# Longer DRAM runs, a weight part on ScalarE, and gathered rows and early blocks moved to another stage, in a one-layer transformer trunk with product-key experts

## The chip, the cores and the metric

The kernel runs on one core of a Trainium2 chip. Its engines work side by side, each through an instruction queue of its own and in order: PE (TensorE, the matmuls, with PEld for its weight loads), DVE (VectorE), ACT (ScalarE), POOL (GpSimd, here the gathers) and SP (SyncE, here the queue of most loads). Sixteen DMA engines move the data. The metric is device microseconds (us) of one execution; the time of a kernel is the median of its runs.

## The reference

One layer over 1024 tokens of width 1024. A norm, one projection, differential attention beside an RG-LRU branch, an output projection, then the part that this change touches, a product-key expert layer (PEER):

```python
q = (xt @ w_query).reshape(T, PEER_HEADS, 2, PEER_HALF)        # 8 heads
s1, s2 = q[:, :, 0] @ sub_keys_1.T, q[:, :, 1] @ sub_keys_2.T   # 128 keys each
v1, i1 = top_k(s1, 16); v2, i2 = top_k(s2, 16)
sc, ci = top_k(all sums v1 + v2, 16)
eid = i1[ci // 16] * 128 + i2[ci % 16]                          # 1 of 16384 experts
g = softmax(sc)
out = sum over (h, k) of g * gelu(expert_down[eid] . xt) * expert_up[eid]
```

Each token so uses 128 of 16384 experts (8 heads, 16 each); `expert_down` and `expert_up` hold 1024 float32 per expert. A last norm follows.

## The kernel before

The 1024 tokens are split in two ways of computing the expert layer. The first 384 (three blocks, `NG = 3`) are **gathered**: POOL fetches one row of an expert table per token and slot (`row`, 128 tokens by 1024, 0.5 MB), and DVE multiplies it (L848 for `expert_down`, L858 for `expert_up`). There are 2 x 3 x 128 = 768 such rows. They are dealt out by hand as filler over the later stages: 45 in the attention of the second group, 30 in its output projection, `G_QRY` in its query stage, `G_OH` in the one-hot stage, and the rest (`G_UP`) in the up stage.

The other 640 tokens (five blocks, `ND = 5`) go **densely** through all 128 blocks of 128 experts, in these stages:

- **query stage**: query projection and the 16 largest keys (DVE, L597 to L601), then `top_k` for each of the five blocks, whose result `turn` transposes on PE (tile `ptk`).
- **one-hot stage**: a table of weights, 640 tokens by 16384 experts. For 16 tokens at a time `one_hots` builds one-hot rows on DVE (`o`, L1087) and multiplies them with the gate, which is split into three bfloat16 parts (`ov`, tile `o1v`, L1091). `weights` multiplies them on PE (tile `pg`, three matmuls per token), ACT copies the result to `st` (L1109), and it goes to DRAM (`gw_d`).
- **up stage**: for each block `e` of experts, `weigh` takes the activations `ga` (640 tokens), multiplies them with the weights `gw` of block `e` read back from DRAM (L1155), and splits the product in two float32r halves. Then 15 matmuls per output half (tile `pu`) add the block's part. `EG = 8` blocks make a group, and each group has two passes (one per output half); in the second pass the eight blocks of the next group are weighed, one after the other.

The activations `ga` come from `down_all(e)`: 48 matmuls (tile `pd`) with the block's `expert_down` weights (`draw`, split to `dh` by ACT, L124, and `dl` by DVE, L125) and a gelu by ACT (L997). Some of these blocks are computed **early**, in the query and one-hot stages, as filler for PE; their `ga` goes to DRAM (`act`) and is loaded again in the up stage. `EARLY` and `EXTRA` say which blocks are early (71 of them), `E_QRY`, `E_TOPK` and `E_OH` how many are handed out per stage, and `HOLD` how many of the last stay in SBUF.

A scheduler sets each engine's order from the program; the rows' DVE instructions are pinned in program order. `gw` has `EQ = 4` blocks per load and two buffers; `uraw` (expert_up) has three buffers.

Of the kernel before, what the change touches and what calls it, by code (L numbers as in the profile page):

```python
# [21 lines left out]
P = 128  # L22
# [21 lines left out]
EG = 8  # L44
EQ = 4
EARLY = 4
TG = 32
TB = 16
TI = 2

G_ATT, G_OUT, G_QRY, G_TOPK, G_OH = 45, 30, 70, 0, 128
G_UP = 2 * NG * SLOTS - (G_ATT + G_OUT + G_QRY + G_TOPK + G_OH)
B_OUT, B_CHAIN, B_TURN, B_QRY, B_TOPK = 0, 3, 8, 8, 12
A_STEPS, A_AHEAD, A_FILL, LRU_AT, WO_AT = 3, 4, 0.5, 0.7, 50
E_QRY, E_TOPK, E_OH = 8, 20, 40
TURN5 = 2
OH_LAST = 96
NORM_IN = ((0,), (1,), (2, 3))
NORM_B = ((0, 1), (2, 3))
HOLD = 2  # L60
PRE = 0
TAIL = 4
RAWS = 4
EXTRA = 8
E_FIRST = 32
# [36 lines left out]
def trunk(  # L102
    ctx: ExitStack,
    tc: tile.TileContext,
    x, norm1_g, w_qk, w_v, w_lru, lam4, subln_g, conv_w, conv_b, w_ra, b_ra, w_ri, b_ri,
    lru_lam, w_out, norm2_g, norm2_c, w_query, keys_t, down_t, expert_down, expert_up, norm_f_g, out,
):
# [872 lines left out]
    def down_all(e, pin=False):  # L980

        ga = dp.tile([P, TD], F32, name="ga", bufs=2 + HOLD + PRE)
        pd = [ps_d.tile([P, 512], F32, name="pd") for _ in range(2)]
        for kh in range(2):
            raw = dp.tile([P, 4, P], F32, name="draw", bufs=RAWS)
            nc.sync.dma_start(raw, down_t[e, :, 4 * kh:4 * kh + 4, :])
            wh = dp.tile([P, 4, P], F32R, name="dh")
            wl = dp.tile([P, 4, P], F32R, name="dl")
            split(raw, wh, wl)
            for c in range(2):  # L990
                sl = slice(c * HT, (c + 1) * HT)
# [14 lines left out]
    with ExitStack() as ph:  # L1006
# [29 lines left out]
        slot_k = [sl_pool.tile([P, P // TI, 2, TI], BF, name=f"slot_k{b}") for b in range(ND)]  # L1036
        slot_w = [sl_pool.tile([P, P // TI, 3, TI], BF, name=f"slot_w{b}") for b in range(ND)]
        ps_t = ph.enter_context(tc.tile_pool(name="ps_k", bufs=2, space=PSUM))
        def turn(b, five):
            pt = ps_t.tile([P, 5, P], BF, name="ptk")  # L1040
            for i in range(5):
                T.transpose(pt[:, i, :], five[:, i, :], ident_b)
            for dst, i, n in ((slot_k[b], 0, 2), (slot_w[b], 2, 3)):
                A.copy(dst.rearrange("p g n i -> p n g i"),
                       pt[:, i:i + n, :].rearrange("p n (g i) -> p n g i", i=TI))

        last = None
# [28 lines left out]
        def one_hots(t0):  # L1076


            b, tt = divmod(t0, P)
            g0 = tt // TI  # L1080

            def per_slot(t, n):
                return t[:, g0:g0 + GB, :, None, :].broadcast_to([P, GB, n, P, TI]).rearrange(
                    "p g n k i -> p (g n) k i")

            o = oh.tile([P, GB, 2, P, TI], BF, name="o21", bufs=3)
            V.tensor_tensor(o.rearrange("p g n k i -> p (g n) k i"),  # L1087
                            key_t[:, None, :, :].broadcast_to([P, GB * 2, P, TI]),
                            per_slot(slot_k[b], 2), op=ALU.is_equal)
            ov = oh.tile([P, GB, 3, P, TI], BF, name="o1v", bufs=OB)  # L1090
            V.tensor_tensor(ov.rearrange("p g n k i -> p g n (k i)"),  # L1091
                            o[:, :, 1:2, :, :].rearrange("p g n k i -> p g n (k i)").broadcast_to(
                                [P, GB, 3, P * TI]),
                            per_slot(slot_w[b], 3), op=ALU.mult)
            return o, ov

        def weights(t0, o, ov):
            if t0 % TG == 0:
                sts[t0 // TG] = st_pool.tile([P, NK, TG], F32, name="st")
            st = sts[t0 // TG]  # L1100
            for t4 in range(0, TB, 4):
                ps = ps_g.tile([P, 4, P], F32, name="pg")
                for t in range(t4, t4 + 4):
                    g, j = divmod(t, TI)
                    for i in range(3):
                        T.matmul(ps[:, t - t4, :], o[:, g, 0, :, j], ov[:, g, i, :, j],  # L1106
                                 start=i == 0, stop=i == 2)
# [23 lines left out]
    with ExitStack() as ph:  # L1131
        up = ph.enter_context(tc.tile_pool(name="up", bufs=2))
        wp = ph.enter_context(tc.tile_pool(name="wp", bufs=EG + 1))
        gp = ph.enter_context(tc.tile_pool(name="gp", bufs=2))
        ps_u = ph.enter_context(tc.tile_pool(name="ps_u", bufs=5, space=PSUM))
# [32 lines left out]
        for g in range(NK // EG):  # L1168
            for second in range(2):
# [100 lines left out]
```

## Time and profile before

| | |
|---|---|
| time, median of 3 runs | 2824.18 us (2811.93 to 2824.65) |
| the profiled execution's own time | 2816.51 us |
| its span, first to last instruction | 2814.6 us |
| PE busy in the span | 2644.4 us (94%) |
| DVE busy | 2336.4 us (83%) |
| ACT busy | 1041.5 us (37%) |
| mean granted TensorE clock | 0.974 |
| moved by DMA | 769.42 MB, mean 273 GB/s |

The stages that the change touches follow one another in the span: the query stage from 677 us to the first transpose of a top-k result at 954.7, the one-hot stage to 1470.9 (the last weight matmul), a switch to the first up matmul at 1509.5, and the up stage to 2803. An engine's busy time is what its instructions cover, and neighbouring matmuls overlap, so a pace is read from the count of matmuls in a stretch, not from the length of one.

### The profile page before, as it was taken

To read this page: it belongs to the slowest core of one execution; us is meant where nothing else is said; L and a number is where in the kernel's file an instruction comes from. 1 tells how busy PE (TensorE), PEld (TensorE's weight loads), DVE (VectorE), ACT (ScalarE), POOL (GpSimd) and SP (SyncE) were. 2 spreads that over 40 slices of the span, in tenths; PEclk is the share of its full clock that TensorE was granted. 3 is DMA by queue.
4 is the path that set the end of the run, shared out by engine and by line. 5 is a ranking of instruction groups with operands and counts; after the bars stand their busy time and mean duration, and the time that the engine had idled before them with its cause. 6 is when DMAs were issued, how large, how long until landed. Compare 5 with 4: busy or idle time off the path is not lost.

```text
span 2814.6 us, 43357 instructions
## 1 busy us (share of the span) xinstructions
PE 2644.4 (94%) x15489; PEld 2318.3 (82%) x15489; DVE 2336.4 (83%) x4838; ACT 1041.5 (37%) x1953; POOL 1119.6 (40%) x906
## 2 busy tenths in 40 slices
PE   7989978898998599999999999999999999999997
PEld 6765966647998599889998888888888888888886
DVE  7553979968999989999995888888888788888888
ACT  5652437824324444344342322222222222222222
POOL 2210035442250305643432444555464444545553
PEclk9999989999999799999999999999999999999999
DMA  6655389775583638888989999999999999999986
GB/s 196 148 140 174 110 200 233 227 266 207 187 291 112 199 105 311 329 297 311 345 320 363 313 324 330 346 338 347 336 332 318 316 336 332 356 340 332 342 292 235
DMA packets 353097, 769.42 MB, mean 273 GB/s; under 512 B 29696, under 2 KB 130064, under 8 KB 350320
## 3 DMA queue, kind: packets, MB, share of 16 engines
q0 software_dynamic: 136432, 425.67, 45.3%
q1 hardware_dynamic: 199488, 274.06, 29.6%
q10 hardware_dynamic: 16960, 66.92, 5.9%
q8 instruction: 121, 1.98, 0.3%
q14 instruction: 96, 0.79, 0.1%
HBM read 681.53 MB, written 85.00 MB: 272 GB/s over the span
## 4 chain that ended last, share of the span: by engine, by line
PE 66%; DVE 12%; issue 9%; DMA 8%; ACT 2%; POOL 2%; SPq 0%; ACTq 0%; POOLq 0%; DVEq 0%
PE pu L144 9%; PE pu L147 9%; PE pu L148 9%; PE pd L148 7%; PE pd L144 7%; PE pd L147 7%; PE pg L1106 3%; DVE row L848 3%; DMA row<-in_expert_down,eid 2%; POOL row L831 2%; PE pp L144 2%; PE pp L147 2%; PE pp L148 2%; PE pa L144 2%; PE pa L147 2%
## 5 line engine op out<-in xcount | busy, mean ns | idle before, releaser
L831 POOL DMA_INDIRECT row<-in_expert_up,eid x384 | 521.7, 1359 | 721.3 <-DVE accg L858 488.0
L831 POOL DMA_INDIRECT row<-in_expert_down,eid x384 | 518.0, 1349 | 548.7 <-DVE row L848 391.0
L144 PE MATMUL pd<-xdH,dh 128*128 128x320 f32 x2048 | 643.2, 315 | 5.3 <-ACT dh L124 3.5
L148 PE MATMUL pd<-xdH,dl 128*128 128x320 f32 x2048 | 628.9, 314 | 14.3 <-DVE dl L125 13.2
L147 PE MATMUL pd<-xdL,dh 128*128 128x320 f32 x2048 | 637.5, 312 | 0.0
L858 DVE SCALAR_TENSOR_TENSOR accg<-row,wg,accg 128x1024 f32<-128x1024 f32 x384 | 491.7, 1280 | 17.9 <-DMA row<-in_expert_up,eid 14.6
L147 PE MATMUL pu<-ul,w_h 128*128 128x512 f32 x1280 | 504.0, 394 | 0.2 <-DVE ul L125 0.2
L148 PE MATMUL pu<-uh,w_l 128*128 128x512 f32 x1280 | 500.3, 393 | 0.0
L848 DVE SCALAR_TENSOR_TENSOR row<-row,x2g 128x1024 f32<-128x1024 f32 x384 | 462.9, 1220 | 18.7 <-DMA row<-in_expert_down,eid 18.2
L148 PEld LDWEIGHTS pd<-xdH,dl 128*128 128x128 f32 x2048 | 386.0, 190 | 23.7 <-DVE dl L125 15.2
L144 PEld LDWEIGHTS pd<-xdH,dh 128*128 128x128 f32 x2048 | 390.0, 190 | 15.9 <-ACT dh L124 4.7
L147 PEld LDWEIGHTS pd<-xdL,dh 128*128 128x128 f32 x2048 | 389.3, 190 | 9.0
L144 PE MATMUL pu<-uh,w_h 128*128 128x512 f32 x1280 | 378.9, 394 | 11.2 <-ACT uh L124 5.8
L124 ACT CAST dh<-draw 128x512 fp32r<-128x512 f32 x256 | 159.0, 622 | 422.8 <-PE pd L147 390.4
L124 ACT CAST uh<-uraw 128x512 fp32r<-128x512 f32 x256 | 158.9, 621 | 416.8 <-PE pu L148 302.9
L147 PEld LDWEIGHTS pu<-ul,w_h 128*128 128x128 f32 x1280 | 242.0, 189 | 48.3 <-DVE ul L125 1.0
L148 PEld LDWEIGHTS pu<-uh,w_l 128*128 128x128 f32 x1280 | 242.1, 189 | 47.3
L144 PEld LDWEIGHTS pu<-uh,w_h 128*128 128x128 f32 x1280 | 236.0, 189 | 54.1 <-ACT uh L124 7.1
L125 DVE TENSOR_TENSOR dl<-draw,dh 128x512 fp32r<-128x512 f32 x256 | 174.6, 688 | 82.0 <-ACT dh L124 72.3
L125 DVE TENSOR_TENSOR ul<-uraw,uh 128x512 fp32r<-128x512 f32 x256 | 175.8, 687 | 42.1 <-ACT uh L124 40.3
L124 ACT CAST w_h<-ga 128x640 fp32r<-128x640 f32 x128 | 93.0, 730 | 260.8 <-PE pu L147 208.6
L997 ACT ACTIVATE ga<-pd 128x320 f32<-128x320 f32 x256 | 110.5, 435 | 142.2 <-PE pd L148 126.6
(262 smaller groups left out, 3948.9 us busy)
## 6 DMA issues: line engine op xcount, KB each, us to landing
draw<-in_down_t SPq DMA_DIRECT2D x256, 256.0 KB
uraw<-in_expert_up SPq DMA_DIRECT2D x256, 256.0 KB
gw<-gw_d SPq DMA_DIRECT2D x32, 1280.0 KB
gw_d<-st ACTq DMA_DIRECT2D x20, 1536.0 KB
act<-ga ACTq DMA_DIRECT2D x69, 320.0 KB
ga<-act SPq DMA_DIRECT2D x69, 320.0 KB
wraw<-in_w_query SPq DMA_DIRECT2D x64, 256.0 KB
gw_d<-st ACTq DMA_DIRECT2D x20, 512.0 KB
```

Source lines behind the costliest of these rows:

```text
L124: A.copy(hi, src)
L125: (eng or V).tensor_sub(lo, src, hi.bitcast(F32))
L144: t = T.matmul(ps, wh, mh, start=first, stop=False)
L147: T.matmul(ps, wh, ml, start=False, stop=False)
L148: T.matmul(ps, wl, mh, start=False, stop=last)
L831: nc.gpsimd.indirect_dma_start(out=r, out_offset=None, in_=table, in_offset=bass.IndirectOffsetOnAxis(ap=eids[tb][:, s:s + 1], axis=0))
L848: tc.keep_in_program_order(V.scalar_tensor_tensor(r, r, 1.0, x2, op0=ALU.mult, op1=ALU.mult, accum_out=act[:, s:s + 1]))
L858: tc.keep_in_program_order(V.scalar_tensor_tensor(acc, r, w[:, s:s + 1], acc, op0=ALU.mult, op1=ALU.add))
L997: A.activation(ga[:, c * HT:(c + 1) * HT], pd[c][:, :HT], AF.Gelu_apprx_tanh)
L1106: T.matmul(ps[:, t - t4, :], o[:, g, 0, :, j], ov[:, g, i, :, j], start=i == 0, stop=i == 2)
```

## The change

- **Gathered rows**: `G_QRY` from 70 to 30 and `G_OH` from 128 to 170, so `G_UP` goes from 495 to 493.
- **Early blocks**: `EARLY` and `EXTRA` make 83 blocks early instead of 71, and `E_OH` hands out 50 instead of 40 in the one-hot stage. One block instead of two stays in SBUF (`HOLD`), and `ga` has one buffer less.
- **Gate part on ScalarE**: two of the three gate parts are still multiplied on DVE; the third is done by 16 ACT instructions per 16 tokens, one per token, each 128 wide (tile `o1a`), with the gate as scale.
- **DRAM runs**: `gw` is loaded for 8 blocks at a time (1 KB runs, 2.5 MB) into one buffer, not for 4 (512 B runs, 1.25 MB) into two. `draw` is one load of 4 KB runs, not two of 2 KB. `uraw` is loaded for two blocks at a time from a copy of `expert_up` laid out for it, in 4 KB runs, with two buffers.

```diff
-EQ = 4
-EARLY = 4
+EQ = 8
+EARLY = 5
-G_ATT, G_OUT, G_QRY, G_TOPK, G_OH = 45, 30, 70, 0, 128
+G_ATT, G_OUT, G_QRY, G_TOPK, G_OH = 45, 30, 30, 0, 170
-E_QRY, E_TOPK, E_OH = 8, 20, 40
+E_QRY, E_TOPK, E_OH = 8, 20, 50
-HOLD = 2
+HOLD = 1
-RAWS = 4
-EXTRA = 8
+RAWS = 2
+EXTRA = 4
...
+        raw = dp.tile([P, KD, P], F32, name="draw", bufs=RAWS)
+        nc.sync.dma_start(raw, down_t[e])
         for kh in range(2):
-            raw = dp.tile([P, 4, P], F32, name="draw", bufs=RAWS)
-            nc.sync.dma_start(raw, down_t[e, :, 4 * kh:4 * kh + 4, :])
...
-            ov = oh.tile([P, GB, 3, P, TI], BF, name="o1v", bufs=OB)
+            ov = oh.tile([P, GB, 2, P, TI], BF, name="o1v", bufs=OB)
...
-            return o, ov
+            oa = oh.tile([P, GB, P, TI], BF, name="o1a", bufs=OB)
+            for t in range(TB):
+                g, j = divmod(t, TI)
+                A.activation(oa[:, g, :, j], o[:, g, 1, :, j], AF.Copy,
+                             scale=slot_a[b][:, tt + t:tt + t + 1])
+            return o, (ov[:, :, 0], ov[:, :, 1], oa)
...
-        gp = ph.enter_context(tc.tile_pool(name="gp", bufs=2))
+        gp = ph.enter_context(tc.tile_pool(name="gp", bufs=1))
...
-                    raw = up.tile([P, 512], F32, name="uraw", bufs=3)
-                    nc.sync.dma_start(raw, expert_up[e * P:(e + 1) * P, sl])
+                    if j % 2 == 0:
+                        raw2 = up.tile([P, 2, 512], F32, name="uraw", bufs=2)
+                        nc.sync.dma_start(raw2, up_h[half, e // 2])
+                    raw = raw2[:, j % 2, :]
...
+        "up_h": a["expert_up"][0].reshape(NK // 2, 2, P, 2, 512).transpose(3, 0, 2, 1, 4),
```

ScalarE's order in the one-hot stage, before, one step of 16 tokens (`dh` and `ga` belong to an early block, `st` to the weight table):

```order
L124 CAST dh<-draw 128x512
L997 ACTIVATE ga<-pd 128x320
L124 CAST dh<-draw 128x512
L997 ACTIVATE ga<-pd 128x320
L1109 COPY st<-pg 128x128x4
L1022 DMA act_15763<-ga 128x640
L1109 COPY st<-pg 128x128x4 x3
```

The same engine and place in the changed kernel:

```order
L124 CAST dh<-draw 128x512
L997 ACTIVATE ga<-pd 128x320
L124 CAST dh<-draw 128x512
L997 ACTIVATE ga<-pd 128x320
L1116 COPY st<-pg 128x128x4
L1022 DMA act_15372<-ga 128x640
L1116 COPY st<-pg 128x128x4 x3
L1100 ACTIVATE o1a<-o_15446,slot_a_8444 128x128 x16
```

Sixteen instructions now stand between the copies of one step and the first cast of the next early block.

VectorE's order in the up stage, before, from the last use of one `gw` buffer (`gw_19164`) to the first use of the load that takes its place (`gw_19861`); between them stands the other buffer, `gw_19720`, and rows and splits are left out:

```order
L1155 TENSOR_TENSOR ga_19394<-ga_19394,gw_19164 128x640
...
L125 TENSOR_TENSOR ul_19527<-uraw_19524,uh_19526 128x512
...
L1155 TENSOR_TENSOR ga_19722<-ga_19722,gw_19720 128x640
L1155 TENSOR_TENSOR ga_19756<-ga_19756,gw_19720 128x640
L125 TENSOR_TENSOR ul_19554<-uraw_19551,uh_19553 128x512
L1155 TENSOR_TENSOR ga_19790<-ga_19790,gw_19720 128x640
...
L1155 TENSOR_TENSOR ga_19863<-ga_19863,gw_19861 128x640
```

The same place in the changed kernel, where `gw_20696` and `gw_21371` take turns in one buffer:

```order
L1162 TENSOR_TENSOR ga_21050<-ga_21050,gw_20696 128x640
...
L125 TENSOR_TENSOR ul_21184<-uraw_21181,uh_21183 128x512
...
L125 TENSOR_TENSOR ul_21209<-uraw_21181,uh_21208 128x512
...
L125 TENSOR_TENSOR ul_21236<-uraw_21233,uh_21235 128x512
L125 TENSOR_TENSOR ul_21261<-uraw_21233,uh_21260 128x512
L125 TENSOR_TENSOR dl_21638<-draw_21635,dh_21637 128x512
L1162 TENSOR_TENSOR ga_21373<-ga_21373,gw_21371 128x640
```

The next `gw` may be asked for only after the first of these rows and is needed at the last, four `ul` (four blocks of up matmuls) later.

SP's queue in the up stage of the changed kernel, from one `gw` load on:

```order
L1151 DMA gw<-gw_d 128x20x256
L1157 DMA ga<-act_10365 128x640
L1189 DMA uraw<-in_up_h 128x1024 x2
L1157 DMA ga<-act_10466 128x640
L1189 DMA uraw<-in_up_h 128x1024
L985 DMA draw<-in_down_t 128x1024
```

Behind each `gw` stand loads of `ga` and `uraw`, as they did before with a `gw` of half the size.

On PE the count of `pd` matmuls ahead of the first `pu` goes from 72.25 to 83.0 blocks of 48.

## Rows read from the trace of the kernel before

**Rows 1.** Windows by stage: length; PE, PEld, DVE, ACT, POOL busy (count); clock, DMA share, GB/s.

```profile
677.00:954.70 277.70, 235.40 (x1600) 232.99 (x1598) 276.86 (x1246) 98.67 (x185) 79.16 (x66) 0.93 0.60 198
954.70:1470.90 516.20, 497.72 (x4442) 485.58 (x4443) 478.97 (x571) 223.18 (x408) 200.56 (x113) 0.97 0.77 278
1470.90:1509.50 38.60, 32.80 (x204) 31.05 (x204) 18.06 (x31) 8.95 (x18) 11.85 (x10) 0.96 1.05 387
1509.50:2803.00 1293.50, 1284.18 (x6516) 1121.22 (x6516) 1080.56 (x1517) 359.26 (x636) 647.81 (x498) 0.99 0.94 328
```

**Rows 2.** PE's waits from 954.7 to 1509.5: total us, times, longest.

```profile
PE ptk L1042 <- DVE five L620: 32.1, 1, 32.1
PE pd L148 <- DVE dl L125: 11.8, 6, 3.9
```

**Rows 3.** Groups on DVE from 677 to 954.7: count, busy us, mean ns.

```profile
L858 DVE SCALAR_TENSOR_TENSOR accg<-row,wg,accg 128x1024 f32<-128x1024 f32 x34 | 43.5, 1280 | 0.0
L848 DVE SCALAR_TENSOR_TENSOR row<-row,x2g 128x1024 f32<-128x1024 f32 x32 | 38.8, 1221 | 0.0
```

**Rows 4.** Windows of one tile's instructions, on unbroken stretches: pd, then pu.

```profile
1019.00:1031.00 12.00, 12.00 (x82) 12.00 (x83) 1.74 (x4) 1.00 0.40 128
...
2132.70:2140.30 7.60, 7.60 (x34) 6.28 (x35) 0.00 (x0) 1.00 0.77 233
```

**Rows 5.** Window of the instructions of pd in the up stage.

```profile
1509.50:2803.00 1293.50, 448.80 (x2676) 420.43 (x2676) 48.62 (x114) 0.99 0.94 328
```

**Rows 6.** Groups on DVE from 954.7 to 1509.5.

```profile
L1091 DVE TENSOR_TENSOR o1v<-o,slot_w 128x6144 bf16<-128x6144 bf16 x40 | 134.2, 3355 | 8.5 <-PE pg L1106 7.9 <-issue 0.6
...
L125 DVE TENSOR_TENSOR dl<-draw,dh 128x512 fp32r<-128x512 f32 x111 | 74.7, 686 | 31.5 <-ACT dh L124 29.2 <-PE pd L148 1.9
```

**Rows 7.** Groups on ACT from 945 to 1509.5.

```profile
L1109 ACT COPY st<-pg 128x512 f32<-128x512 f32 x160 | 93.0, 588 | 48.8 <-PE pg L1106 36.6 <-issue 2.5 <-DVE five L620 1.2
L124 ACT CAST dh<-draw 128x512 fp32r<-128x512 f32 x111 | 69.0, 622 | 176.2 <-PE pd L147 162.7 <-DMA draw<-in_down_t 6.4 <-DMA uraw<-in_expert_up 5.4
L997 ACT ACTIVATE ga<-pd 128x320 f32<-128x320 f32 x110 | 47.9, 436 | 77.3 <-PE pd L148 72.8 <-issue 4.4
...
L1057 ACT CAST five<-gate_d 128x128 bf16<-128x128 f32 x9 | 2.7, 298 | 3.8 <-DVE gate_d L1059 3.8
```

**Rows 8.** PE's waits in the up stage, 1510 to 2803.

```profile
PE pu L144 <- ACT uh L124: 5.8, 4, 3.1
PE pu L144 <- DVE acc L1205: 3.2, 1, 3.2
```

**Rows 9.** DVE's longest wait there.

```profile
DVE ga L1155 <- DMA ga<-act: 46.8, 13, 9.2
```

**Rows 10.** Timeline of SP's queue, 1930 to 1966: start, us of issue, load.

```profile
1936.88 0.37 SPq L1144 DMA_DIRECT2D gw<-gw_d  x1
1939.91 9.15 SPq L1150 DMA_DIRECT2D ga<-act  x1
...
1956.30 0.38 SPq L1144 DMA_DIRECT2D gw<-gw_d  x1
1956.90 6.10 SPq L986 DMA_DIRECT2D draw<-in_down_t  x1
```

**Rows 11.** The same queue, 2010 to 2042.

```profile
2013.28 0.38 SPq L1144 DMA_DIRECT2D gw<-gw_d  x1
2015.21 11.02 SPq L1150 DMA_DIRECT2D ga<-act  x1
...
2033.73 0.38 SPq L1144 DMA_DIRECT2D gw<-gw_d  x1
2035.44 3.04 SPq L1181 DMA_DIRECT2D uraw<-in_expert_up  x2
```

**Rows 12.** DMA queues from 1960 to 1965: packets, MB, share of 16 engines.

```profile
q1 hardware_dynamic: 2549, 1.40, 105.2%
```

**Rows 13.** DMA queues from 1510 to 2780.

```profile
q0 software_dynamic: 71424, 260.08, 56.9%
```

More of the change, by code (lines that the diff above doesn't have):

```diff
@@ L105, in trunk @@
     x, norm1_g, w_qk, w_v, w_lru, lam4, subln_g, conv_w, conv_b, w_ra, b_ra, w_ri, b_ri,
-    lru_lam, w_out, norm2_g, norm2_c, w_query, keys_t, down_t, expert_down, expert_up, norm_f_g, out,
+    lru_lam, w_out, norm2_g, norm2_c, w_query, keys_t, down_t, expert_down, expert_up, up_h, norm_f_g, out,
 ):
@@ L983, in down_all @@
         pd = [ps_d.tile([P, 512], F32, name="pd") for _ in range(2)]
+        raw = dp.tile([P, KD, P], F32, name="draw", bufs=RAWS)
+        nc.sync.dma_start(raw, down_t[e])
         for kh in range(2):
-            raw = dp.tile([P, 4, P], F32, name="draw", bufs=RAWS)
-            nc.sync.dma_start(raw, down_t[e, :, 4 * kh:4 * kh + 4, :])
             wh = dp.tile([P, 4, P], F32R, name="dh")
             wl = dp.tile([P, 4, P], F32R, name="dl")
-            split(raw, wh, wl)
+            split(raw[:, 4 * kh:4 * kh + 4, :], wh, wl)
             for c in range(2):
@@ L1036, in trunk @@
         slot_k = [sl_pool.tile([P, P // TI, 2, TI], BF, name=f"slot_k{b}") for b in range(ND)]
-        slot_w = [sl_pool.tile([P, P // TI, 3, TI], BF, name=f"slot_w{b}") for b in range(ND)]
+        slot_w = [sl_pool.tile([P, P // TI, 2, TI], BF, name=f"slot_w{b}") for b in range(ND)]
+        slot_a = [sl_pool.tile([P, P], F32, name=f"slot_a{b}") for b in range(ND)]
         ps_t = ph.enter_context(tc.tile_pool(name="ps_k", bufs=2, space=PSUM))
@@ L1042, in turn @@
                 T.transpose(pt[:, i, :], five[:, i, :], ident_b)
-            for dst, i, n in ((slot_k[b], 0, 2), (slot_w[b], 2, 3)):
+            for dst, i, n in ((slot_k[b], 0, 2), (slot_w[b], 2, 2)):
                 A.copy(dst.rearrange("p g n i -> p n g i"),
                        pt[:, i:i + n, :].rearrange("p n (g i) -> p n g i", i=TI))
+            A.copy(slot_a[b], pt[:, 4, :])
         last = None
@@ L1089, in one_hots, with weights @@
                             per_slot(slot_k[b], 2), op=ALU.is_equal)
[L1090 removed]
+            ov = oh.tile([P, GB, 2, P, TI], BF, name="o1v", bufs=OB)
             V.tensor_tensor(ov.rearrange("p g n k i -> p g n (k i)"),
                             o[:, :, 1:2, :, :].rearrange("p g n k i -> p g n (k i)").broadcast_to(
[L1093 to L1097 removed]
+                                [P, GB, 2, P * TI]),
+                            per_slot(slot_w[b], 2), op=ALU.mult)
+            oa = oh.tile([P, GB, P, TI], BF, name="o1a", bufs=OB)
[4 more added lines that the diff above has]
+            return o, (ov[:, :, 0], ov[:, :, 1], oa)
+        def weights(t0, o, parts):
             if t0 % TG == 0:
@@ L1104, in weights @@
                     g, j = divmod(t, TI)
-                    for i in range(3):
-                        T.matmul(ps[:, t - t4, :], o[:, g, 0, :, j], ov[:, g, i, :, j],
+                    for i, part in enumerate(parts):
+                        T.matmul(ps[:, t - t4, :], o[:, g, 0, :, j], part[:, g, :, j],
                                  start=i == 0, stop=i == 2)
```

## The prediction

> **What bounds the kernel now.** I read the windows by stage first, because the engine that sets the pace changes from stage to stage [rows 1]. In the query stage (677 to 954.7 us) DVE is busy for 276.86 of 277.7 us and PE for 235.4: DVE sets the pace. PE's one long wait, 32.1 us, is for the last result that DVE makes there, `five` of the first top-k [rows 2]. In the one-hot stage and the switch after it (554.8 us together) PE is busy for 497.7 + 32.8 = 530.5 us and DVE for 479.0 + 18.1 = 497.1: both are nearly full, PE a little more. In the up stage PE is busy for 1284.2 of 1293.5 us, and its waits come to about 9 us [rows 8], so PE sets the pace there and nothing else matters until it makes PE wait. The DMA engines work at a share of 0.94 in that stage, so they are the next in line.
>
> Paces come from counts in unbroken stretches [rows 4]: 82 `pd` matmuls in 12.0 us are 0.147 us each, so a block of 48 is 7.05 us; 34 `pu` matmuls in 7.6 us are 0.224 us each, so the 15 of one block and half are 3.35 us. The up stage holds 2676 `pd` [rows 5] and 2 x 128 x 15 = 3840 `pu`: 393 + 860 = 1253 us of its 1293.5.
>
> The sum is made against the profiled execution, 2816.5 us. The median of the runs shown, 2824.2, is 7.7 us above it; 0.5% (14 us) is about what a measurement of this kernel can tell from no change.
>
> **Query stage: 40 rows fewer.** A row costs DVE 1.22 us (`expert_down`) or 1.28 us (`expert_up`) [rows 3], so 40 rows are 49 to 51 us. DVE is full, so its end of the stage comes 50 us earlier, but PE then becomes the limit: it has 235.4 us of work in 277.7, which leaves 42 to be won. I take 40. The number of early blocks on PE there is the same as before. The bounds are 0, if the top-k chain and not the rows holds the transposes back, and 50.
>
> **One-hot stage and switch: work comes in.**
> PE: ahead of the first `pu` stand 83.0 blocks of `pd` for 72.25, so 10.75 x 7.05 = 75.8 us come in. PE idles 554.8 - 530.5 = 24.3 us now. If the new work fills all of that, the stage grows by 51.5 us; if none, by 75.8. The granted clock of 0.97 means that some 16 us of its time are lost to the lower of the two clock levels (1.2 for 2.4 GHz), so with PE never idle the growth could be 35. I take 52.
> DVE: 42 more rows are 42 x 1.25 = 52.5 us; the splits of 10.75 more blocks are 21.5 x 0.686 = 14.7 us; the third gate part takes a third of 40 instructions of 3.355 us away, 44.7 us [rows 6]. Sum +22.5: 519.6 us of work, below the 606 us of PE. DVE stays close, not first.
> ACT: the 640 new instructions of 128 elements are not in the trace. The nearest row is a cast of 128 elements, 298 ns [rows 7], so 190.7 us; a far upper bound is the strided copy of 512 elements, 588 ns, so 376 us. I take the cast, since length and types are its own. ACT is busy for 223.2 + 9.0 = 232.1 us; with 10.75 blocks at 2 x 0.622 + 2 x 0.436 = 2.1 us, 22.7, it comes to 446 of 606 us. It is in order, however: a burst of sixteen (4.8 us) now stands ahead of each cast `dh`. PE has a whole block of 7.05 us of `pd`, cast before the burst, to work on meanwhile, so I take nothing for it. Without that cover the burst costs up to 4.8 us in each of 40 steps.
> On the move of that part the row says 3.355 / 3 = 1.12 us on DVE against 16 x 0.298 = 4.8 us on ACT for the same 16 tokens. By the row the dearer place is free, since ACT would still be idle for 160 us. The Trainium skill (ScalarE: Activation LUTs, Rules for kernel authors) says to do multiplications on VectorE, not on ScalarE; left on DVE the part would give DVE 564 us, still under PE's 606, so by the rule the move gains nothing and brings only the risk of the burst.
>
> **Up stage: work goes out, and one buffer.** 10.75 blocks less are -75.8 us of a PE that is full. Shorter waits on transfers can give back at most the 9 us of PE's waits, so the longer runs of `uraw` and `draw` get nothing by themselves. The one buffer of `gw` is the new wait. SP stands still behind each `gw` until the DMA rings have taken it: in four cases the next issue ended 12.2, 6.7, 13.0 and 4.8 us after the issue of `gw` began [rows 10, 11], for 1.25 MB in 2560 runs. The new load has 2.5 MB in 2560 runs, so it takes 5 to 26 us: no longer if the runs count, twice as long if the bytes count. It can be asked for after the last use of the old `gw` and is needed four up blocks later by the order: 4 x 3.35 = 13.4 us and about 36 `pd` between them, 5.3 us, make 18.7. Only the slowest case is late, by 7 us. In that time DVE and everything queued behind its wait stand still: rows, the splits `ul`, the sums; PE has one or two split blocks left, 3.4 to 6.7 us. DVE waits already, for the `ga` that stands behind `gw` on SP, 46.8 us in 13 waits [rows 9], and PE did not feel it. I take 1 us for each of 15 loads, 15 us; the bounds are -9 and 15 x 7.3 = 110 us.
> The DMA engines: at 0.94 of 1293.5 us they work 1216 us, and the stage is to have 1233. 512-byte runs take 5 us x 1.052 x 16 / 2549 = 33 ns [rows 12]; 4 KB runs take at most 1270 x 0.569 x 16 / 63488 = 182 ns, when all but the 63,488 row packets are counted as nothing [rows 13]. Between them I estimate 53 ns for 1 KB, so 40,960 in place of 81,920 runs free 169 - 136 = 33 us. Eleven blocks less to load and 13 activations more to fetch nearly cancel. So they stay at a share of about 0.96.
>
> **Edits at nothing.** `draw` in one piece lets the first cast start after 512 KB, not 256 KB, about 0.8 us later at 328 GB/s; 48 matmuls of the block before cover it, and without that it would be 0.8 x 128 = 100 us. One `ga` buffer less delays the loads of `ga`; PE's cover is the same as for `gw`. The copies `slot_a` are five.
>
> The sum: -40 + 52 - 76 + 15 = -49, so 2816.5 - 49 = 2768 us.
>
> **The rivals.**
> (1) *The single `gw` buffer makes PE wait in each group: slower.* For it: the load doubles, DMA has a share of 0.94, and DVE is in order. Against it: DVE's waits of up to 9.2 us [rows 9] did not reach PE. At 7.3 us a group the sum is 2768 - 15 + 110 = 2863. It decides from (49 + 15) / 15 = 4.3 us of PE wait per load. The Trainium skill (Trainium Kernel Development and Optimization, Best Practices) says to double-buffer so that DMA overlaps with compute; this case is that rule broken. Chance 0.16.
> (2) *ACT's burst paces the one-hot stage.* For it: in-order ACT, both casts and PSUM copies behind sixteen instructions. Against it: 160 us of slack. With the upper price ACT has 631 us, 25 more than PE, so 2793. Chance 0.12.
> (3) *The query stage gives nothing back*, since PE waits for top-k results by its order, and their chain through DVE and ACT is as long. Against it: DVE is never idle there. 2768 + 40 = 2808. Chance 0.10.
> (4) *DMA sets the up stage.* For it: a share of 0.94 now, and rows and `uraw` late at a higher one. Against it: neither DVE nor PE waits long for either today. If the share can't rise above 0.94, the 1216 - 33 us of engine time need 1258 us in place of 1233, 25 more: 2793. Chance 0.10.
> My forecast has 0.52.
>
> **How the numbers follow.** The forecast's own range is 2740 to 2800: one-hot growth of 35 to 76 and -9 to +15 for `gw`. Cases 2 and 4 stay faster by 0.5%, case 3 lies at the border (below 2810 is faster, against the median). Case 1 is slower in three of four. Faster 0.52 + 0.12 + 0.08 = 0.72; slower 0.13; same 0.15. The range, 2738 to 2838, leaves out most of case 1 and a little below.
>
> **What would show it.** Query stage: the transposes `ptk` start about 40 us earlier and PE's 32.1 us wait is nearly gone. One-hot: about 607 us to the first `pu`, PE idle for under 25 us, `o1a` at about 0.3 us, `o1v` at 2.24. Up: about 1233 us, PE's waits under 25 us. It is wrong if PE shows a new wait on `ul` or `uh` behind DVE's wait for `gw` in each group, if `o1a` takes over 0.4 us and PE waits for `dh` after each burst, or if the first `ptk` does not move.

## The result, and the profile after

The changed kernel takes 2861.4 us (median of 4 runs, 2859.71 to 2863.09) against 2824.41 us before (4 runs, 2811.93 to 2828.01). The ratio is 1.0139 with a 95% interval of 1.0107 to 1.0171: 1.4% slower, and above the forecast range. The profiled execution has a span of 2860.0 us, 45.4 us more than before.

The windows of the changed kernel by stage, columns as in [rows 1]: query stage, one-hot stage, switch, two pieces of the up stage, and what follows the last up matmul.

```profile
680.00:918.70 238.70, 231.53 (x1599) 229.94 (x1597) 234.11 (x1182) 98.05 (x183) 33.63 (x29) 0.99 0.45 144
918.70:1484.50 565.80, 558.02 (x4923) 546.81 (x4923) 490.90 (x640) 416.49 (x1094) 214.47 (x147) 1.00 0.81 300
1484.50:1524.80 40.30, 36.09 (x242) 35.09 (x240) 19.83 (x36) 12.23 (x24) 9.47 (x9) 1.00 1.04 398
1524.80:2716.00 1191.20, 1159.26 (x5757) 1001.83 (x5758) 959.88 (x1359) 318.27 (x553) 579.48 (x439) 0.99 0.91 323
2716.00:2779.50 63.50, 58.81 (x245) 46.17 (x243) 56.80 (x67) 16.41 (x36) 42.68 (x32) 0.97 0.89 314
2779.50:2860.00 80.50, 0.00 (x0) 0.00 (x0) 61.02 (x116) 1.87 (x4) 44.65 (x35) 0.52 0.77 275
```

The last row has no counterpart in the forecast: for 80.5 us PE does nothing at all. Before, 11.4 us followed the last up matmul. The stages, taken between the first `pd`, the first `ptk`, the first `pu` and the last `pu`, read so:

| us | before | predicted change | after | measured change |
|---|---|---|---|---|
| up to the first `pd` | 677.9 | 0 | 680.6 | +2.7 |
| query stage | 276.9 | -40 | 238.1 | -38.8 |
| one-hot stage and switch | 554.8 | +52 | 606.1 | +51.3 |
| up stage | 1293.7 | -61 | 1254.5 | -39.2 |
| after the last up matmul | 11.4 | 0 | 80.7 | +69.3 |
| sum | 2814.7 | -49 | 2860.0 | +45.3 |

Two numbers are off, by 22 us in the up stage and by 69 us behind it. The timeline of the changed kernel behind the last up matmul (start, duration, engine, operation, and in brackets what ended the idle time before it) shows what fills the end:

```profile
2778.96 0.39 PE L148 MATMUL pu<-uh,w_l 128*128 128x512 f32 x1
...
2786.32 1.54 POOL L831 DMA_INDIRECT row<-in_expert_up,eid  x1 [0.30 <-issue]
2787.47 1.28 DVE L858 SCALAR_TENSOR_TENSOR accg<-row,wg,accg 128x1024 f32<-128x1024 f32 x1 [0.43 <-DMA row<-in_expert_up,eid]
2788.16 1.41 POOL L831 DMA_INDIRECT row<-in_expert_up,eid  x1 [0.30 <-issue]
2789.15 1.29 DVE L858 SCALAR_TENSOR_TENSOR accg<-row,wg,accg 128x1024 f32<-128x1024 f32 x1 [0.39 <-DMA row<-in_expert_up,eid]
...
2827.95 0.94 POOL L831 DMA_INDIRECT row<-in_expert_up,eid  x1 [1.15 <-DVE accg L858]
```

Gathered rows: 37 of the 768 are still to be multiplied when PE ends (none before). The last starts at 2841.4 us, so they take 63.2 us, 1.71 us each, at the pace of the gathers: POOL is busy for 44.65 us with 35 instructions there, and 0.30 us of issue stands between two, together 1.58 us a row.

They stand there by VectorE's own order, which the scheduler fixes before the run. The trace has 45 rows behind the last split `ul` of the changed kernel (the first line ends with it), and one before (the two lines below it). From VectorE's timeline, after and then before:

```profile
2766.26 1.28 DVE L125 TENSOR_TENSOR ul<-uraw,uh 128x512 fp32r<-128x512 f32 x2
```

```profile
2789.14 0.69 DVE L125 TENSOR_TENSOR ul<-uraw,uh 128x512 fp32r<-128x512 f32 x1 [1.17 <-ACT uh L124]
2789.75 1.28 DVE L858 SCALAR_TENSOR_TENSOR accg<-row,wg,accg 128x1024 f32<-128x1024 f32 x1
```

In the up stage the new waits are these, in the list of waits from 1525 to 2779 (us, times, longest):

```profile
PE pd L148 <- DVE dl L125: 15.9, 9, 3.3
PE pu L147 <- DVE ul L125: 9.6, 10, 1.8
PE pd L144 <- ACT dh L124: 7.4, 5, 2.6
...
DVE ga L1162 <- DMA gw<-gw_d: 115.2, 15, 11.6
```

DVE waits for each of the 15 `gw` loads, 7.7 us on the average, where before it waited longest for the `ga` that stood behind `gw` on SP [rows 9]; that wait is down to 0.2 us. Around one load, first SP's queue and then DVE in the timeline:

```profile
2098.34 0.88 SPq L1151 DMA_DIRECT2D gw<-gw_d  x1
2100.27 14.84 SPq L1157 DMA_DIRECT2D ga<-act  x1
...
2112.51 0.69 DVE L125 TENSOR_TENSOR ul<-uraw,uh 128x512 fp32r<-128x512 f32 x1 [2.11 <-ACT uh L124]
2121.78 1.56 DVE L1162 TENSOR_TENSOR ga<-ga,gw 128x640 f32<-128x640 f32 x2 [8.57 <-DMA gw<-gw_d]
```

SP's next issue ends at 2115.11, 16.8 us after `gw`'s began [rows 10 and 11 had 5 to 13 us], and the data are there for DVE at 2121.78, 23.4 us after it. The loads stand in the chain that ended last with 9% of the span, and in the page's list of transfers (count, KB each, median us from issue to landing) so:

```profile
gw<-gw_d SPq DMA_DIRECT2D x16, 2560.0 KB, 21.4
```

### The profile page after: what moved, and what is told of

It reads as the page before. It is cut to its first block, busy times and chain, and to the rows that moved or that the text cites. A ratio compares the mean times of both kernels' runs of the same rounds, so it can differ in the third digit from the quotient of the medians.

```text
span 2860.0 us, 43412 instructions
## 1 busy us (share of the span) xinstructions
PE 2640.8 (92%) x15489; PEld 2309.6 (81%) x15489; DVE 2293.6 (80%) x4838; ACT 1213.5 (42%) x2598; POOL 1103.9 (39%) x906
## 4 chain that ended last, share of the span: by engine, by line
PE 48%; DMA 19%; issue 15%; DVE 10%; POOL 5%; ACT 3%; DVEq 0%; SPq 0%; POOLq 0%; ACTq 0%
DMA gw<-gw_d 9%; PE pd L148 6%; PE pd L144 6%; PE pd L147 5%; POOL row L831 5%; PE pu L147 4%; DMA row<-in_expert_down,eid 4%; PE pu L148 4%; PE pu L144 4%; PE pg L1113 3%; DVE row L848 2%; DMA row<-in_expert_up,eid 2%; PE pa L144 2%; PE pa L148 2%; PE pa L147 2%
## 5 line engine op out<-in xcount | busy, mean ns | idle before, releaser
L831 POOL DMA_INDIRECT row<-in_expert_down,eid x384 | 506.2, 1318 | 695.2 <-DVE row L848 532.8
L144 PE MATMUL pu<-uh,w_h 128*128 128x512 f32 x1280 | 386.2, 393 | 5.7 <-ACT uh L124 3.4
L1162 DVE TENSOR_TENSOR ga<-ga,gw 128x640 f32<-128x640 f32 x128 | 103.6, 821 | 117.8 <-DMA gw<-gw_d 115.2
## 6 DMA issues: line engine op xcount, KB each, us to landing
gw<-gw_d SPq DMA_DIRECT2D x16, 2560.0 KB, 21.4
```

The lines of the kernel that those rows point to most:

```text
L144: t = T.matmul(ps, wh, mh, start=first, stop=False)
L831: nc.gpsimd.indirect_dma_start(out=r, out_offset=None, in_=table, in_offset=bass.IndirectOffsetOnAxis(ap=eids[tb][:, s:s + 1], axis=0))
L1162: V.tensor_tensor(gv, gv, gw[:, :, j * TG:(j + 1) * TG], op=ALU.mult)
```

## The experiments

**Theories.** (A) Rows are late: the shortened up stage can't take the rows that are left for it, and they run behind it. (B) The single `gw` buffer makes PE and the rows wait, and the end comes of that. The rivals are that the move of work into the one-hot stage, the part on ACT or the runs cost something themselves. Within A, the up stage may be short of DVE time or of DMA throughput. Ratios are to the kernel before in the same session; its medians there were 2814.3, 2815.5 and 2816.8 us, up to 10 us below the 2824.4 of the result, so kernels of different sessions are compared by their ratios. The stages and rows are those of one traced execution each. "Late" rows are those begun behind the last up matmul.

| kernel | median us | ratio (95%) | query | one-hot, switch | up | end | rows done at first `pu` / late |
|---|---|---|---|---|---|---|---|
| before | 2824.41 | 1 | 276.9 | 554.8 | 1293.7 | 11.4 | 265 / 0 |
| after | 2861.40 | 1.0139 (1.0107 to 1.0171) | 238.1 | 606.1 | 1254.5 | 80.7 | 260 / 37 |
| e1, two `gw` buffers | 2827.62 | 1.0046 (1.0035 to 1.0057) | 238.1 | 605.3 | 1217.9 | 81.8 | 260 / 38 |
| e2, rows back | 2884.48 | 1.0236 (1.0203 to 1.0269) | 278.2 | 620.9 | 1247.8 | 56.5 | 277 / 23 |
| e3, early blocks back | 2844.34 | 1.0103 (1.0074 to 1.0131) | 238.1 | 541.9 | 1329.6 | 56.9 | 234 / 24 |
| e4, before, rows alone | 2826.19 | 1.0036 (1.0021 to 1.0051) | 238.2 | 564.3 | 1292.8 | 51.6 | 237 / 21 |
| e5, e6 and a sixth row buffer | 2831.64 | 1.0047 (1.0026 to 1.0068) | 238.1 | 606.5 | 1291.9 | 14.5 | 260 / 0 |
| e6, e1, `uraw` per block | 2855.84 | 1.0170 (1.0121 to 1.0219) | 238.2 | 609.5 | 1248.8 | 70.9 | 260 / 32 |
| e7, gate on DVE | 2889.27 | 1.0268 (1.0234 to 1.0301) | 238.1 | 632.6 | 1256.1 | 80.1 | 260 / 37 |
| e8, e1, rows 70 and 170 | 2818.75 | 1.0017 (0.9997 to 1.0036) | 277.7 | 641.2 | 1196.7 | 11.4 | 314 / 0 |
| e9, e5, half of a row on DVE | 2799.87 (1 run) | | 234.5 | 613.3 | 1278.8 | 11.4 | 265 / 0 |
| e10, e9, half of a row fetched | 2756.39 (1 run) | | 234.5 | 625.4 | 1215.3 | 11.4 | 279 / 0 |
| e11, e1, rows still earlier | 2821.66 | 1.0008 (0.9989 to 1.0027) | 238.9 | 626.6 | 1221.0 | 13.2 | 302 / 0 |
| e12, before, long runs alone | 2817.09 | 0.9995 (0.9979 to 1.0012) | 277.6 | 555.5 | 1286.1 | 11.4 | 260 / 0 |

**e1: two `gw` buffers.** The changed kernel with `gw` as it was before.

```diff
-EQ = 8
+EQ = 4
-        gp = ph.enter_context(tc.tile_pool(name="gp", bufs=1))
+        gp = ph.enter_context(tc.tile_pool(name="gp", bufs=2))
```

> The changed kernel with gw loaded for 4 blocks into two buffers again. Theory A (rows): the end is set by gathered rows that the order of the up stage has not placed; its order still leaves 47 rows behind the last split of expert_up (46 in the changed kernel), so the tail behind the last up matmul stays at about 80 us. PE gets back its waits behind gw, some 30 us: about 2830 us. Theory B (gw): DVE's 115 us of waits for gw delay rows and PE both; without them the rows catch up too, the tail falls to some 12 us and the time to about 2765 us.

The up stage falls from 1254.5 to 1217.9 us, by 36.6, and the end stays. Its windows of the up stage and the end:

```profile
1525.70:2743.60 1217.90, 1204.54 (x6000) 1043.22 (x6000) 1017.48 (x1425) 337.94 (x589) 606.59 (x469) 1.00 0.94 333
2743.60:2825.40 81.80, 0.00 (x0) 0.00 (x0) 62.34 (x117) 1.87 (x4) 44.91 (x36) 0.52 0.77 275
```

PE is idle for 13.4 us of the up stage; after, with 6002 matmuls in the two pieces shown above, for 1254.7 - 1159.3 - 58.8 = 36.6 us. That is 23 of the 36.6; the rest is the same matmuls being busy 13.5 us longer, at a granted clock of 0.99 (0.97 in the last piece) against 1.00. Theory A's forecast came out (2827.6 us for 2830, and the end stays); theory B's end of 12 us did not. What holds of B is the price of the single buffer in the up stage, 36.6 us. Its loads also had runs of 1 KB, not of 512 B; the two were undone together.

**e2: rows back.** The changed kernel with the rows dealt as before.

```diff
-G_ATT, G_OUT, G_QRY, G_TOPK, G_OH = 45, 30, 30, 0, 170
+G_ATT, G_OUT, G_QRY, G_TOPK, G_OH = 45, 30, 70, 0, 128
```

> The changed kernel with 70 rows in the query stage and 128 in the one-hot stage, as before. Theory A (rows): the query stage takes its 39 us again; 31 instead of 46 rows are left behind the last split, at 1.7 us each 25 us less of tail: about 2870 us, no better than the change. Theory B (gw): the rows were no cause, the time is that of the change plus the query stage's 39 us, 2900 us.

Of the 40 us that the query stage takes more, the one-hot stage gives nothing back; it is 15 us longer, though DVE has 22 rows fewer in it. One part of that is a block of 48 `pd` matmuls more (3264 for 3216), 7 us that its up stage then has less. PE's idle time grows by 1.8 us only. The rest, some 6 us, goes with the granted clock, 0.98 on the average for 1.00. Its low stretch is the start of the stage, right behind the wait of [rows 2], which ends the query stage again. The wait, then the first 43 us of the one-hot stage in e2 and in the changed kernel:

```profile
PE ptk L1043 <- DVE five L620: 29.2, 1, 29.2
```

```profile
956.70:1000.00 43.30, 39.30 (x261) 39.03 (x262) 42.23 (x132) 30.93 (x70) 3.65 (x3) 0.90 0.35 114
```

```profile
918.70:962.00 43.30, 41.35 (x289) 40.41 (x289) 42.54 (x136) 31.33 (x73) 0.24 (x1) 1.00 0.32 107
```

Neither theory's time came out (2870 and 2900; it is 2884), but A's shorter end did. There are 14 fewer late rows and 24 us less behind the last matmul, but the 40.1 us of the query stage and 14.8 of the one-hot stage weigh more. So moving the 40 rows is no loss in the changed kernel: undoing it costs some 23 us (ratios 1.0236 and 1.0139).

**e3: early blocks back.** The changed kernel with the 71 early blocks of before, its other parts kept.

```diff
-EARLY = 5
+EARLY = 4
-E_QRY, E_TOPK, E_OH = 8, 20, 50
+E_QRY, E_TOPK, E_OH = 8, 20, 40
-EXTRA = 4
+EXTRA = 8
```

> The changed kernel with 71 early blocks again (71 in place of 83). Theory A (rows): the up stage is 76 us longer for PE, one-hot 51 us shorter; the longer up stage takes more rows, 32 are left behind it, 24 us less of tail: about 2862 us. Theory B (gw): the tail stays, so the time rises by 76 - 51 = 25 us to about 2885 us.

The one-hot stage and switch give 64.2 us back, the up stage takes 75.1 more: the blocks pay 11 us between the two, less than the forecast's 75.8 - 52 = 24, but they pay. But without them the end is 23.8 us shorter, 24 late rows for 37, since the longer up stage takes more of them: 510 rows run in it for 471. That is theory A's end (24 us less); its time, 2862 us, was not met, since the one-hot stage gave back 64 us and not 51. In all, the traced execution with the early blocks is 17 us longer, 4.4 us of it ahead of the first `pd`. By the ratios, 1.0139 and 1.0103, it is some 10 us, and their intervals overlap: the late rows take back what the early blocks win, and a net loss is not shown.

**e4: the move of the rows alone**, on the kernel before.

```diff
-G_ATT, G_OUT, G_QRY, G_TOPK, G_OH = 45, 30, 70, 0, 128
+G_ATT, G_OUT, G_QRY, G_TOPK, G_OH = 45, 30, 30, 0, 170
```

> The kernel before with the rows alone moved (30 in the query stage, 170 in the one-hot stage). Theory A (rows): the query stage is 38 us shorter, but 29 rows in place of 2 are left behind the last split, some 48 us of tail, and the one-hot stage grows a little for the rows it takes: 2820 to 2845 us, slower. Theory B (gw): nothing waits for gw here, so the query stage's gain stays but for a little of the one-hot stage: about 2790 us.

The query stage gives its 38.7 us, the one-hot stage takes 9.5 and the end 40.2. Up to and with the one-hot stage 45 + 30 + 30 + 170 = 275 rows are dealt out, and 237 are done at the first `pu`: 38 of them pass on into an up stage of the old length, 1292.8 us, which takes 510 and leaves 21. Before, 265 of 273 were done there. A number in the table of rows says when a row is handed out, not when it runs. The time lies in theory A's range; B's 2790 us is out.

**e5 and e6: a sixth row buffer for the up stage.** Both are e1 with `uraw` loaded per block as before; e5 has the sixth buffer as well (`MORE = 1`), from the space that this frees.

```diff
+            taken[0] += 1
+            pool = rows if not more or taken[0] % (5 + MORE) < 5 else more[0]
-            r = rows.tile([P, D], F32, name="row")
+            r = pool.tile([P, D], F32, name="row")
...
+        more.append(ph.enter_context(tc.tile_pool(name="rows_x", bufs=MORE)))
...
-                    if j % 2 == 0:
-                        raw2 = up.tile([P, 2, 512], F32, name="uraw", bufs=2)
-                        nc.sync.dma_start(raw2, up_h[half, e // 2])
-                    raw = raw2[:, j % 2, :]
+                    raw = up.tile([P, 512], F32, name="uraw", bufs=3)
+                    nc.sync.dma_start(raw, expert_up[e * P:(e + 1) * P, sl])
```

> The changed kernel with gw in two buffers of 4 blocks, expert_up loaded per block again (three buffers of 2 KB), and the 2 KB so freed used for a sixth row buffer in the up stage. Theory A1 (row cycle): each gathered row holds one of five buffers from its gather to its DVE instruction, and that, not DVE or the transfers, limits the rows that the up stage takes; the order now leaves 5 rows in place of 47 behind the last split, so the tail falls from 82 to about 22 us with the up stage at about 1220: 2765 us. Theory A2 (DVE or DMA is full): the rows only wait longer for their transfers or push PE's splits back; up stage and tail together stay at about 1300 us: 2820 us.

> The same with five row buffers, so that only the runs of expert_up differ from the kernel with two gw buffers (2827.6 us). Theory A1: 40 in place of 47 rows are left behind the last split, 12 us less tail: 2816 us, up stage unchanged at 1218. Rival (long runs matter): without the 4 KB runs the transfers are slower, the up stage grows by its DMA share, some 20 us: 2845 us.

With the sixth buffer no row is late, but the up stage is 43 us longer than e6's, which itself is 31 us longer than e1's. Up stage and end together are 1306.4 us (e5), 1319.7 (e6) and 1299.7 (e1): the rows are no longer late, and most of their cost has moved in front of the last matmul. VectorE's order has changed: 4 rows stand behind its last `ul`, for 39 in e6. The wait that carries the cost, in the lists of PE's waits in the up stages of e5 and of e6:

```profile
PE pu L144 <- ACT uh L124: 58.7, 22, 8.4
```

```profile
PE pu L144 <- ACT uh L124: 27.3, 17, 5.7
```

`uh` in turn waits for the loads of `uraw`, here for ACT in e5:

```profile
ACT uh L124 <- DMA uraw<-in_expert_up: 181.0, 38, 13.8
```

So the row buffers set how many rows the order places in the stage, and the stage that takes them all has another limit. Theory A2's sum came out (about 1300 us). Against e6, which differs by the buffer alone, the buffer wins 13 us of these two and 24 us of the median. The sixth buffer beside loads of two blocks was not tried. Of e6's expectations, A1's shorter end (11 us less) and the rival's longer stage both came out.

**e7: all three gate parts on DVE** as before, the rest of the change kept.

```diff
-            ov = oh.tile([P, GB, 2, P, TI], BF, name="o1v", bufs=OB)
+            ov = oh.tile([P, GB, 3, P, TI], BF, name="o1v", bufs=OB)
...
-            oa = oh.tile([P, GB, P, TI], BF, name="o1a", bufs=OB)
-            for t in range(TB):
-                g, j = divmod(t, TI)
-                A.activation(oa[:, g, :, j], o[:, g, 1, :, j], AF.Copy,
-                             scale=slot_a[b][:, tt + t:tt + t + 1])
...
```

> The changed kernel with all three gate parts on VectorE. Theory A: PE is the limit of the one-hot stage, DVE has 564 us of work in its 606, so the stage stays at about 606 to 615 and the order leaves the same 46 rows behind: 2860 to 2870 us. Rival D (the part on ScalarE is what lets PE fill the stage): the stage takes the 45 us again: 2905 us.

The one-hot stage and switch grow from 606.1 to 632.6 us, the other stages stay within 2 us. Its window there:

```profile
914.80:1547.40 632.60, 602.90 (x5163) 589.22 (x5162) 552.98 (x673) 253.52 (x473) 291.61 (x154) 0.98 0.81 296
```

DVE is busy for 553 of 633 us and yet PE loses 26.5. Of that, 17.7 us are idle time (29.7 for 12.0) and 8.8 a longer busy time at a clock of 0.98. Theory A's 606 to 615 us are out, and rival D gets 26.5 of its 45. The largest new wait is for VectorE's product, which the changed kernel does not wait for:

```profile
PE pg L1106 <- DVE o1v L1091: 8.8, 3, 4.5
```

**e8: e1 with rows 70 and 170**, so that 40 rows fewer are left for the up stage.

```diff
-G_ATT, G_OUT, G_QRY, G_TOPK, G_OH = 45, 30, 30, 0, 170
+G_ATT, G_OUT, G_QRY, G_TOPK, G_OH = 45, 30, 70, 0, 170
```

> The changed kernel with gw in two buffers of 4 blocks and 70 rows in the query stage beside 170 in the one-hot stage (40 less in the up stage). Theory A: query stage 277 us again, one-hot and switch 606 to 620, up stage 1218, no rows left behind it, tail 12: 2790 to 2805 us. Rival B (the rows are no bound, only work on DVE): the tail was due to the late start of the up stage; time as with two gw buffers plus the query stage's 39 us: 2866 us.

```profile
1594.50:2791.20 1196.70, 1193.88 (x5953) 1032.80 (x5952) 1009.62 (x1402) 337.27 (x587) 585.11 (x451) 1.00 0.93 329
2791.20:2802.60 11.40, 0.00 (x0) 0.00 (x0) 7.12 (x31) 0.72 (x2) 0.00 (x0) 0.67 0.46 185
```

The end is 11.4 us as before, and PE is busy for all but 2.8 us of the up stage: on the rows A holds. Its time does not (2790 to 2805 expected), for the one-hot stage and switch take 641 us and not 606 to 620. Against e1 the stage and the end win 91.6 us; the query stage takes 39.6 and the one-hot stage 35.9 (7 us of that win and of the 35.9 are one block of `pd` that has moved from the up stage to the one-hot stage). Most of the 35.9 is the switch, 63.9 us for 40.1, with PE idle for 16.6; why was not followed. That leaves a kernel as fast as the one before (its profiled execution is the fastest of its ten, 2804.57 us; the median is 2818.75).

**e9 and e10: DVE or DMA?** Both are e5 with less done per row: in e9 DVE multiplies 512 of the 1024 columns and the transfers stay; in e10 only 512 are fetched, too. Both leave out half of the row work.

```diff
-                        r, r, 1.0, x2, op0=ALU.mult, op1=ALU.mult, accum_out=act[:, s:s + 1]))
+                        r[:, :512], r[:, :512], 1.0, x2[:, :512], op0=ALU.mult, op1=ALU.mult, accum_out=act[:, s:s + 1]))
...
-                        acc, r, w[:, s:s + 1], acc, op0=ALU.mult, op1=ALU.add))
+                        acc[:, :512], r[:, :512], w[:, s:s + 1], acc[:, :512], op0=ALU.mult, op1=ALU.add))
```

```diff
-                out=r, out_offset=None, in_=table,
+                out=r[:, :512], out_offset=None, in_=table.rearrange("n (two d) -> (n two) d", two=2),
```

> The kernel with six row buffers, where each gathered row is fetched whole but VectorE multiplies only its first 512 of 1024 columns (half of the row work is left out, the transfers are whole). Up stage there so far: 1291.9 us, with PE waiting 59 us for casts of expert_up that wait for their loads. Theory A2-DMA (the DMA engines are full at a share of 0.94 to 0.96): the up stage stays at 1270 to 1295 us. Theory A2-DVE (VectorE's row work is what delays PE): it falls to 1195 to 1220 us.

> The same, and only 512 columns of each row are fetched (2 KB instead of 4 KB; half of the row work is left out). Both theories: up stage 1195 to 1215 us, PE's floor being 1191; under A2-DMA it is this step and not the one before that brings it down, and the DMA share falls to about 0.7.

The up stages in windows, e5, e9 and e10, each from its own trace:

```profile
1524.40:2816.30 1291.90, 1227.58 (x6000) 1052.38 (x6000) 1068.94 (x1502) 336.91 (x591) 676.47 (x503) 0.98 0.93 329
```

```profile
1507.70:2786.50 1278.80, 1222.75 (x6000) 1053.35 (x6000) 813.54 (x1500) 336.17 (x591) 547.82 (x497) 0.98 0.93 329
```

```profile
1527.40:2742.70 1215.30, 1198.22 (x5954) 1034.05 (x5952) 795.19 (x1464) 333.43 (x585) 519.23 (x483) 1.00 0.74 234
```

Taking 255 us of work from DVE shortens the stage by 13.1 us, with PE still waiting for `uh` (42.9 us in 15 waits), and the rate stays at 329 GB/s. Taking half of the rows' bytes away as well shortens it by another 63.5, and that wait falls to 2.7 us. (Not all of this is the stage's own: e9 has 5 rows fewer in it than e5 and e10 another 14, at 1.7 us a row 8.5 of the 13.1 and 24 of the 63.5; e10 also has one block of `pd` fewer in it, 7 us.) Both stages lie where A2-DMA put them, e10's on the edge. The up stage that takes all its rows is short of DMA throughput. Both are single executions. Those of e5 lie within 14 us, so the 13.1 may be nothing; the 63.5, with 40 us less of that wait, is far outside.

**e11: e1 with rows still earlier**, 20 more in the attention and 10 more in the output projection.

```diff
-G_ATT, G_OUT, G_QRY, G_TOPK, G_OH = 45, 30, 30, 0, 170
+G_ATT, G_OUT, G_QRY, G_TOPK, G_OH = 65, 40, 30, 0, 170
```

> The changed kernel with gw in two buffers of 4 blocks, and 30 rows moved from the up stage to the stages ahead of the query stage (65 in the attention, 40 in the output projection). Theory A (the up stage holds some 460 rows at PE's pace, the rest is paid for): up stage about 1205 us, tail 12 to 15, the earlier stages 10 to 38 us longer: 2755 to 2785 us. Rival (rows cost the same wherever they stand): the 30 rows cost 38 us ahead and save no more than the 40 us of tail that they took: 2820 us.

The end is 13.2 us, but the first `pd` comes 34.3 us later than in e1 and the one-hot stage is 21.3 us longer; the time is that of before. The rival's 2820 us came out, not theory A's 2755 to 2785: here the rows moved to the earlier stages cost nearly what they save at the end.

**e12: long runs alone**, on the kernel before (`uraw` for two blocks, `draw` in one piece, `HOLD = 1`).

```diff
-            raw = dp.tile([P, 4, P], F32, name="draw", bufs=RAWS)
-            nc.sync.dma_start(raw, down_t[e, :, 4 * kh:4 * kh + 4, :])
+        raw = dp.tile([P, KD, P], F32, name="draw", bufs=RAWS)
+        nc.sync.dma_start(raw, down_t[e])
...
-                    raw = up.tile([P, 512], F32, name="uraw", bufs=3)
-                    nc.sync.dma_start(raw, expert_up[e * P:(e + 1) * P, sl])
+                    if j % 2 == 0:
+                        raw2 = up.tile([P, 2, 512], F32, name="uraw", bufs=2)
+                        nc.sync.dma_start(raw2, up_h[half, e // 2])
+                    raw = raw2[:, j % 2, :]
```

> The kernel before with the 4 KB runs of expert_up (two blocks per load) and of the expert_down weights alone, one held block instead of two to make room. Theory A: PE is full in the up stage of before (1267 of 1294 us of matmuls), so at most 9 to 20 us are to be had: 2800 to 2815 us. Rival (two splits more in stock and shorter transfers are worth the 30 us that the changed kernel loses without them): 2785 us.

Nothing: 0.9995. In the changed kernel with two `gw` buffers the loads of `uraw` for two blocks are worth 31 us of the up stage (e6 against e1; e6 also has three buffers of one block in place of two of two, so longer runs and more blocks in stock are not told apart). PE's wait for `uh` is the difference that shows, 27.3 us in e6 and 3.3 in e1. Theory A's range (2800 to 2815) is missed by 2 us, the rival's 2785 by 32.

## Why the prediction was wrong

**What bounds the kernel** was read rightly stage by stage, and so were two of the three terms that depend on it alone: the query stage (-40, measured -38.8; PE's wait of 32.1 us for `five` is gone) and the one-hot stage (+52, measured +51.3). The second is partly luck: PE's idle time fell by 12.3 us and not by all of its 24.3, and its busy time grew by 63.6 us and not by 75.8, with the granted clock at 1.00 for 0.97. The two misses cancel.

**The step that failed is the one that isn't there.** The sum goes from query to one-hot to up stage and stops; it takes for granted that the rows end with the last matmul, as before, and so puts the change in what follows that matmul at nothing. It measured +69 us. The sum never asks how many rows the up stage takes. The trace of before had a good estimate: 265 rows were done at the first `pu`, so 503 ran in 1293.7 us, one per 2.57 us, beside DMA engines at a share of 0.94. At that pace a stage of 1217.9 us takes 474. e1, which has that length, took 470. After took 471 in 1254.5 us, no more in a stage 36.6 us longer: the count is set by VectorE's order, which was there to be read before the run (46 rows behind the last split as e1's text counts them, 45 in the trace). The change leaves 508 for it (493 dealt to the stage and 15 of the earlier ones that were late already). So 37 come behind the last matmul, at 1.71 us, 63 us. e8 shows it from the other side: with 454 rows left, the end is as short as before. Where the order places all rows in the stage, with a sixth buffer (e5), their time is paid in front of the last matmul, and there it is a matter of DMA throughput and not, for the most part, of DVE (e9 against e10): the long windows of before, e1, e5 and e8 all lie between 328 and 333 GB/s, and in e5 PE waits for loads at that rate.

**The single `gw` buffer**: the mechanism was right and its size was not. I took 1 us of PE per load; it is 36.6 / 15 = 2.4 us (e1), which is 21.6 us more and all of the up stage's error. The working took 18.7 us of cover against 5 to 26 us of load as late only in the slowest case. The loads land 21.4 us after their issue (the median of 16), so nearly each one is late, and DVE stands 7.7 us in each; it reached its wait some 14 us behind the issue, not 18.7. That SP stands still until the rings have taken a load was my reading; the rows show how long the next issue lasts, and not why. Against my bound of 7.3 us, though, PE felt a third of it. On rival (1): it gave 2863 us, and the time is 2861.4, but by another way; at 2.4 us per load the buffer alone would have left the forecast at 2790. The Trainium skill (Trainium Kernel Development and Optimization, Best Practices) asks for double-buffering so that DMA overlaps with compute; e1 agrees, by 36.6 us of the up stage.

**"The longer runs get nothing by themselves"** holds on the kernel before (e12). In the changed kernel it doesn't: with `uraw` loaded per block the up stage is 31 us longer (e6 against e1), by shorter runs or by fewer blocks in stock.

**Rival (4), DMA sets the up stage**, was the nearest to the truth and was mispriced. The share of the up stage did not rise above 0.95 in any kernel with whole rows. I let that lengthen the stage by 25 us. Where all rows are placed in it, it is 74 us longer (e5 against e1, 31 of them from the loads of `uraw`); in the changed kernel the order of DVE has rows behind the last matmul instead, for 69 us.

**The part on ACT**: rival (2) is out. `o1a` and `o1v` in the one-hot stage and switch, in groups as in [rows 6, 7]:

```profile
L1100 ACT ACTIVATE o1a<-o,slot_a 128x128 bf16<-128x128 bf16 x640 | 194.6, 430 | 1.6 <-issue 1.3 <-DVE o L1089 0.3
```

```profile
L1093 DVE TENSOR_TENSOR o1v<-o,slot_w 128x4096 bf16<-128x4096 bf16 x40 | 91.6, 2292 | 7.2 <-PE pg L1113 7.1
```

Each `o1a` lasts 430 ns, over the 0.4 us that I named as the sign of trouble, but they overlap: 194.6 us in all, against the 190.7 that I took. PE waits for `dh` for 1.9 us only. I had the move gain nothing, because DVE's 564 us would still be below PE's 606. e7 measured the part left on DVE: 26.5 us slower in that stage. The Trainium skill (ScalarE: Activation LUTs, Rules for kernel authors) says to do multiplications on VectorE; e7 does not agree. VectorE is busy for 87% of that stage, and PE still waits for its product; comparing sums of busy time doesn't show it.

**The early blocks** do what the sum says between one-hot and up stage, but by shortening the up stage they take room from the rows; so that a gain of 11 us is gone with the 24 us at the end (e3). That ties the failed step to the change: it is the same 75.8 us that I booked as gain.

**What would make it wrong**, in the forecast's own list, named the query stage, ACT and `gw`, and only `gw` came. No sign in it concerned the end of the kernel. The forecast's own range, 2740 to 2800, does not follow from the ends it names either: growth of 35 to 76 and -9 to +15 for `gw` give 2726 to 2791.

What stays open: what sets the pace of the rows in the one-hot stage, where neither PE's work nor the count dealt explains it (155 rows in 606 us after, 132 in 564 in e4, 129 in 542 in e3); their place is fixed by DVE's order, and another order was not tried. Nor was a split of the rows found that beats the kernel before: e8 and e11 equal it. The single buffer was not tried alone on the kernel before, and what besides the row buffers made the scheduler place the rows as it did was not looked into.

## What to carry to other kernels

Filler work has a pace, like the engine that it fills beside: before a stage is shortened, count how much of the filler ran in it, divide by its length, and ask where the remainder goes, for behind the last matmul it costs its whole time. Where a scheduler fixes the order, the remainder can be counted in that order before anything runs. A table that deals work out says when it is offered; when it ran is read from the trace. And a queue that other loads share makes a single buffer dearer than the transfer: cover has to be compared with the typical time from issue to landing under load, not with the chance that it is slow.

## What the runs showed of the hardware

- Whole rows beside dense loads, the sixteen DMA engines moved 327 to 333 GB/s in the up stage of every kernel with two `gw` buffers, at a share of 0.93 to 0.95; neither a sixth row buffer (e5) nor half of the rows' work on DVE (e9) raised that.
- Short waits cost PE more than their length: with 23 us more idle time (after against e1), the same matmuls were busy for another 13.5 us at a granted clock of 0.99, and in e5 for 23.0 us at 0.98.
- ACT's 128-wide instructions each last 430 ns and yet take 304 ns each of its time (194.6 us for 640), since they overlap.
